# Row softmax in one arena: one queue with tiles that grow from 3 to 31 rows, and GpSimd in place of SyncE waiting for the last stores

## The chip, the cores and the metric

The kernel runs on one core of one Trainium2 chip. The metric is the time on the device in microseconds (us). Before the change it was 163.44 us (median of 3 runs, 163.35 to 163.72). Profiled spans are about 1.8 us shorter than these times, because they run from the first to the last instruction of the core.

## The reference

```python
batch, seq, dim = 16, 1024, 512            # x: float32
x_scaled = x / 2.0
x_max = np.max(x_scaled, axis=-1, keepdims=True)
exp_x = np.exp(x_scaled - x_max)
return exp_x / np.sum(exp_x, axis=-1, keepdims=True)
```

These are 16384 rows of 512 values. On 128 partitions each partition has 128 rows of 2 KB. The input and the output are 33.55 MB each; nothing can be left out of the 67.11 MB that pass the DMA engines.

## The kernel before

A "tile" is one load and, later, one store of r rows on each partition, so one packet of r x 2 KB per partition. Its chunks are the pieces that VectorE and ScalarE work on. A tile's second number is its place in the arena of on-chip memory. A tile whose place overlaps an earlier tile's is loaded late, when that tile's store has landed.

```python
PLAN = [
    ([3], 0), ([4, 3], 3), ([5] * 3, 10), ([5] * 3, 25), ([5] * 3, 40), ([5] * 3, 55),
    ([5] * 3, 70), ([5] * 3, 85), ([5] * 3, 10), ([4, 3], 3), ([3], 0), ([3], 25),
]
ARENA = 100
LAG = 2
# ... (cut)
    def do_max(k):                              # VectorE: one reduce per chunk, waits for the load
        # ...
        )._wait_ge(ld[t], 16).then_inc(s_max, 1)
    def do_mul(k):                              # VectorE: reciprocal, then one multiply per row
        # ...
    def compute_and_store():
        # ... ScalarE: one exp per row, with the row's sum
        for k in range(len(chunks) + LAG):
            if k < len(chunks):
                do_max(k)
            if k >= LAG:
                do_mul(k - LAG)

        late = sorted(behind)
        for t in range(len(tiles)):
            nc.sync.wait_ge(s_mul, last_chunk[t] + 1)
            nc.sync.dma_start(out=dram(of, t), in_=sb(t)).then_inc(st[t], 16)
            while late and max(behind[late[0]]) <= t - 1:
                u = late.pop(0)
                for v in behind[u]:
                    nc.sync.wait_ge(st[v], 16)
                nc.sync.dma_start(out=sb(u), in_=dram(xf, u)).then_inc(ld[u], 16)
        for t in range(len(tiles)):
            nc.sync.wait_ge(st[t], 16)
```

All 24 DMAs (12 loads, 12 stores) go through SyncE's queue in program order. The first eight loads (100 rows) are issued at once; stores queue behind them.

The softmax here doesn't subtract the row's maximum and nothing guards it: scores larger than these inputs give would overflow.

Of the kernel before, what the change touches and what calls it, by code (L numbers as in the profile page):

```python
# [1 line left out]

# [4 lines left out]




PLAN = [
    ([3], 0), ([4, 3], 3), ([5] * 3, 10), ([5] * 3, 25), ([5] * 3, 40), ([5] * 3, 55),
    ([5] * 3, 70), ([5] * 3, 85), ([5] * 3, 10), ([4, 3], 3), ([3], 0), ([3], 25),
]
ARENA = 100
LAG = 2


@with_exitstack
def kernel(  # L20
    ctx: ExitStack,
    tc: tile.TileContext,
    x: bass.AP,
    out: bass.AP,
):
    nc = tc.nc
    fp32 = mybir.dt.float32

    xf = x.flatten_outer_dims()
    of = out.flatten_outer_dims()  # L30
    N, D = xf.shape
    P = nc.NUM_PARTITIONS
    n_rows = N // P
    assert sum(sum(c) for c, _ in PLAN) == n_rows

    arena = nc.alloc_sbuf_tensor("arena", (P, ARENA, D), fp32)
    negmax = nc.alloc_sbuf_tensor("negmax", (P, n_rows), fp32)
    sums = nc.alloc_sbuf_tensor("sums", (P, n_rows), fp32)
    recip = nc.alloc_sbuf_tensor("recip", (P, n_rows), fp32)



    tiles, chunks, base = [], [], 0
    for t, (cs, at) in enumerate(PLAN):
        r = sum(cs)
        tiles.append((base, r, at))
        o = 0
        for c in cs:
            chunks.append((t, base + o, c, at + o))
            o += c  # L50
        base += r
    last_chunk = {c[0]: k for k, c in enumerate(chunks)}

    def dram(ap, t):
        b, r, _ = tiles[t]
        return ap[b * P : (b + r) * P].rearrange("(p r) d -> p r d", r=r)

    def sb(t):
        _, r, at = tiles[t]
        return arena[:, at : at + r, :]  # L60


    behind = {}
    for t, (_, r, at) in enumerate(tiles):
        for u in range(t):
            _, ru, au = tiles[u]
            if at < au + ru and au < at + r:
                behind.setdefault(t, []).append(u)

    ld = [tc.alloc_semaphore(f"ld{t}") for t in range(len(tiles))]  # L70
    st = [tc.alloc_semaphore(f"st{t}") for t in range(len(tiles))]
    s_max = tc.alloc_semaphore("s_max")
    s_exp = tc.alloc_semaphore("s_exp")
    s_rec = tc.alloc_semaphore("s_rec")
    s_mul = tc.alloc_semaphore("s_mul")



    def issue_loads(begin, end):
        for t in range(begin, end):  # L80
            if t not in behind:
                nc.sync.dma_start(out=sb(t), in_=dram(xf, t)).then_inc(ld[t], 16)

    def do_max(k):
        t, b, c, a = chunks[k]
        nc.vector.reduce_max(  # L86
            out=negmax[:, b : b + c],
            in_=arena[:, a : a + c],
            axis=mybir.AxisListType.X,
            negate=True,  # L90
        )._wait_ge(ld[t], 16).then_inc(s_max, 1)

    def do_mul(k):
        t, b, c, a = chunks[k]
        nc.vector.reciprocal(  # L95
            out=recip[:, b : b + c], in_=sums[:, b : b + c]
        )._wait_ge(s_exp, k + 1).then_inc(s_rec, 1)
        for r in range(c):
            ins = nc.vector.tensor_scalar_mul(  # L99
                out=arena[:, a + r],  # L100
                in0=arena[:, a + r],
                scalar1=recip[:, b + r : b + r + 1],
            )
            if r == 0:
                ins._wait_ge(s_rec, k + 1)
        ins.then_inc(s_mul, 1)

    def compute_and_store():

        for k, (t, b, c, a) in enumerate(chunks):  # L110
            for r in range(c):
                ins = nc.scalar.activation(  # L112
                    out=arena[:, a + r],
                    in_=arena[:, a + r],
                    func=mybir.ActivationFunctionType.Exp,
                    bias=negmax[:, b + r : b + r + 1],
                    scale=0.5,
                    accum_out=sums[:, b + r : b + r + 1],
                )
                if r == 0:  # L120
                    ins._wait_ge(s_max, k + 1)
            ins.then_inc(s_exp, 1)
# [5 lines that stand above are left out]
            if k >= LAG:  # L128
                do_mul(k - LAG)

        late = sorted(behind)
        for t in range(len(tiles)):
            nc.sync.wait_ge(s_mul, last_chunk[t] + 1)
            nc.sync.dma_start(out=dram(of, t), in_=sb(t)).then_inc(st[t], 16)
            while late and max(behind[late[0]]) <= t - 1:
                u = late.pop(0)
                for v in behind[u]:
                    nc.sync.wait_ge(st[v], 16)
                nc.sync.dma_start(out=sb(u), in_=dram(xf, u)).then_inc(ld[u], 16)
        for t in range(len(tiles)):  # L140
            nc.sync.wait_ge(st[t], 16)



    hook = nc.inst_callbacks[-1]
    nc.remove_inst_callback(hook)
    symbolic = nc._always_lower_symbolic_ap
    nc._always_lower_symbolic_ap = False
    here = str(nc.cur_bb)
    entry = nc.main_func.blocks[0]  # L150
    head, jumps = entry.instructions[:-5], entry.instructions[-5:]
    entry.instructions = []
    nc.switch_bb("main", None)
    issue_loads(0, 2)
    first = list(entry.instructions)
    at = next(k for k, i in enumerate(head) if type(i).__name__ == "InstDrain")
    entry.instructions = head[:at] + first + head[at:]
    issue_loads(2, len(tiles))
    compute_and_store()
    entry.instructions = list(entry.instructions) + jumps  # L160
    nc.switch_bb(here, None)
    nc._always_lower_symbolic_ap = symbolic
    nc.push_inst_callback(hook)


# [1 line left out]
_INS = ['x']  # L167
_OUTS = [((16, 1024, 512), 'float32')]


# [23 lines left out]
```

## Time and profile before

| | before |
|---|---|
| time, median | 163.44 us |
| profiled span | 161.6 us |
| VectorE / ScalarE busy | 126.1 / 94.5 us |
| DMA moved | 67.14 MB, mean 416 GB/s |
| DMA packets | 3460 |

From the profile page of the kernel before. The rows of digits are 40 slices of the span, each the busy tenths of 4.04 us; GB/s is what the DMA engines moved in that slice. Below them are the chain of work that ended last and one group of instructions (count, busy time, mean ns of one, idle time before them and what ended it).

```profile
span 161.6 us, 513 instructions
...
## 2 busy tenths in 40 slices
DVE  0484599999999999999999999999999999100000
...
DMA  7999999999999997999999899999999999999992
GB/s 291 465 403 449 441 418 464 395 458 395 464 411 436 449 411 254 444 438 472 418 434 464 388 431 406 445 456 388 461 441 456 395 464 395 464 411 456 390 410 90
DMA packets 3460, 67.14 MB, mean 416 GB/s; under 512 B 385, under 2 KB 385, under 8 KB 1153
...
## 4 chain that ended last, share of the span: by engine, by line
DVE 74%; DMA 10%; issue 0%; DVEq 0%
...
L86 DVE TENSOR_REDUCE negmax<-arena 128x5 f32<-128x2560 f32 (+2 forms) x28 | 72.3, 2586 | 10.8 <-DMA arena<-in_x_dram 10.8
```

The DMA row is at 9 almost throughout, while VectorE stops before the end (the zeros at the right of its row). The windows view says how fast the DMA is. Its columns are the stretch, its length, busy time of VectorE, ScalarE and GpSimd, the TensorE clock, DMA share and GB/s.

```profile
32.00:58.00 26.00, 25.82 (x36) 19.20 (x54) 0.00 (x0) 1.00 1.01 433
57.00:65.00 8.00, 7.93 (x12) 5.42 (x15) 0.00 (x0) 1.00 0.94 336
70.00:100.00 30.00, 29.79 (x44) 22.25 (x63) 0.00 (x0) 1.00 1.00 430
100.00:140.00 40.00, 37.49 (x63) 26.20 (x72) 0.00 (x0) 1.00 1.01 436
140.00:155.00 15.00, 0.00 (x0) 0.00 (x0) 0.00 (x0) 1.00 0.97 416
158.00:160.00 2.00, 0.00 (x0) 0.00 (x0) 0.00 (x0) 1.00 0.22 89
```

The three longest stretches are at 430 to 436 GB/s. The stretch 140:155 reads 416; the view counts a packet whole at its start, and on the median engine a store of 15 rows landed 9.07 us after the one before it (141.48 and 150.55 us), which is 434 GB/s there too. The stretch 57:65 is slower, and the last 2 us before 160 hold only stragglers. The Trainium skill ("DMA: Bandwidth & Descriptors", Specifications) gives 435 GB/s as the ceiling of the fabric, and this trace lies on it. So the DMA queue is the limit.

The chain of waits has another answer, and must be read with care. These are its last pieces (start, length, what):

```profile
137.06 0.40 DVEq L189
137.45 0.40 DVE arena L99
```

It ends at 137.85 us, although the span is 161.6 us. The chain follows instructions, and the last instruction that counts as work is VectorE's. The 24 us of stores after it are in no chain.

The trace also records when each of the 16 DMA engines finished its part of a DMA ("landing"). For the last store the median engine landed at 158.49 us and the last one at 160.48 us. The remaining 1.09 us is SyncE's wait and the closing barrier of all engines.

### The profile page before, as it was taken

The numbers are of one execution on the slowest core, as the hardware profiler recorded it, in microseconds if no ns is written. First come the engines' busy times: TensorE is split into PE (matmuls) and PEld (weight loads), VectorE is DVE, ScalarE is ACT, GpSimd is POOL, SyncE is SP. The second block draws the span as 40 slices with busy tenths as digits, with TensorE's granted clock in tenths as the row PEclk, the third lists the DMA queues.
The fourth block names the chain that finished last, engine by engine and source line by source line (L and its number), as shares of the span: only waits on it lengthen the run. The fifth ranks groups of instructions, "written<-read, shape, count | busy, mean of one in ns | idle before, by whom it ended". The sixth has DMA issues, their size and how long they took to land.

```text
span 161.6 us, 513 instructions
## 1 busy us (share of the span) xinstructions
DVE 126.1 (78%) x184; ACT 94.5 (59%) x257; POOL 0.2 (0%) x4
## 2 busy tenths in 40 slices
DVE  0484599999999999999999999999999999100000
ACT  3439087866688666797666886667978655000000
POOL 0000000000000000000000000000000000000000
DMA  7999999999999997999999899999999999999992
GB/s 291 465 403 449 441 418 464 395 458 395 464 411 436 449 411 254 444 438 472 418 434 464 388 431 406 445 456 388 461 441 456 395 464 395 464 411 456 390 410 90
DMA packets 3460, 67.14 MB, mean 416 GB/s; under 512 B 385, under 2 KB 385, under 8 KB 1153
## 3 DMA queue, kind: packets, MB, share of 16 engines
q1 hardware_dynamic: 3456, 67.11, 97.7%
q14 instruction: 4, 0.02, 0.0%
HBM read 33.55 MB, written 33.55 MB: 415 GB/s over the span
## 4 chain that ended last, share of the span: by engine, by line
DVE 74%; DMA 10%; issue 0%; DVEq 0%
DVE negmax L86 40%; DVE arena L99 32%; DMA arena<-in_x_dram 10%; DVE recip L95 2%; DVEq L189 0%
## 5 line engine op out<-in xcount | busy, mean ns | idle before, releaser
L112 ACT ACTIVATE arena<-arena,negmax 128x512 f32<-128x512 f32 x128 | 90.7, 710 | 40.1 <-DVE negmax L86 40.1
L86 DVE TENSOR_REDUCE negmax<-arena 128x5 f32<-128x2560 f32 (+2 forms) x28 | 72.3, 2586 | 10.8 <-DMA arena<-in_x_dram 10.8
L99 DVE TENSOR_SCALAR arena<-arena,recip 128x512 f32<-128x512 f32 x128 | 53.2, 482 | 1.0
L112 ACT ACTIVATION_READ_ACCUMULATOR arena<-arena,negmax 128x1 f32 x128 | 23.9, 187 | 0.0
L95 DVE RECIPROCAL recip<-sums 128x5 f32<-128x5 f32 (+2 forms) x28 | 5.0, 177 | 0.0
L112 ACT ACT_TABLE_LOAD x1 | 1.3, 1283 | 1.3 <-PEq L178 1.3
L178 POOL MEMSET const-bfloat16-1.0<- 128x1 bf16 x1 | 0.1, 101 | 0.0
L178 POOL MEMSET const-uint8-127<- 128x1 uint8 x1 | 0.1, 101 | 0.0
L178 POOL MEMSET const-float32-0.0<- 128x1 f32 x1 | 0.1, 98 | 0.2 <-issue 0.2
L178 POOL MEMSET const-float32-1.0<- 128x1 f32 x1 | 0.1, 98 | 0.0
## 6 DMA issues: line engine op xcount, KB each, us to landing
arena<-in_x_dram SPq DMA_DIRECT2D x7, 3840.0 KB, 33.7
out_dram<-arena SPq DMA_DIRECT2D x7, 3840.0 KB, 33.2
arena<-in_x_dram SPq DMA_DIRECT2D x2, 1792.0 KB, 15.2
out_dram<-arena SPq DMA_DIRECT2D x2, 1792.0 KB, 33.2
arena<-in_x_dram SPq DMA_DIRECT2D x3, 768.0 KB, 23.5
out_dram<-arena SPq DMA_DIRECT2D x3, 768.0 KB, 22.6
```

The lines of the kernel that those rows point to most:

```text
L86: nc.vector.reduce_max(out=negmax[:, b : b + c], in_=arena[:, a : a + c], axis=mybir.AxisListType.X, negate=True,)._wait_ge(ld[t], 16).the ...
L95: nc.vector.reciprocal(out=recip[:, b : b + c], in_=sums[:, b : b + c])._wait_ge(s_exp, k + 1).then_inc(s_rec, 1)
L99: ins = nc.vector.tensor_scalar_mul(out=arena[:, a + r], in0=arena[:, a + r], scalar1=recip[:, b + r : b + r + 1],)
L112: ins = nc.scalar.activation(out=arena[:, a + r], in_=arena[:, a + r], func=mybir.ActivationFunctionType.Exp, bias=negmax[:, b + r : b + r ...
L178: nc = _bacc.Bacc("TRN2", target_bir_lowering=False, num_devices=1)
```

## The change

The intent, as it can be read from the change: fewer and larger DMAs (18 instead of 24), tiles that grow so that VectorE's early loads come in time, a written-out queue order, two larger late tiles instead of four small ones, and a shorter end, as the engine that leads the closing barrier waits itself.

```diff
 PLAN = [
-    ([3], 0), ([4, 3], 3), ([5] * 3, 10), ([5] * 3, 25), ([5] * 3, 40), ([5] * 3, 55),
-    ([5] * 3, 70), ([5] * 3, 85), ([5] * 3, 10), ([4, 3], 3), ([3], 0), ([3], 25),
+    ([3], 0), ([5], 3), ([5, 4], 8), ([5] * 3, 17), ([7] * 3, 32), ([8, 8, 8, 7], 53),
+    ([5] * 3, 84), ([6, 6, 5], 0), ([4] * 3, 17),
 ]
-ARENA = 100
+ARENA = 99
+QUEUE = [
+    ("load", 0), ("load", 1), ("load", 2), ("load", 3), ("load", 4), ("load", 5),
+    ("load", 6), ("store", 0), ("store", 1), ("store", 2), ("store", 3), ("load", 7),
+    ("store", 4), ("load", 8), ("store", 5), ("store", 6), ("store", 7), ("store", 8),
+]
 ... (cut: do_queue walks this list on SyncE: a load waits for the stores it lies behind, a store for
      its last chunk; stores that no load waits for share one semaphore, s_end)
-        for t in range(len(tiles)):
-            nc.sync.wait_ge(st[t], 16)
+    for u, sem in [*st.items(), ("end", s_end)]:
+        nc.gpsimd.wait_ge(sem, stored[u])
```

More of the change, by code (lines that the diff above doesn't have):

```diff
@@ L11 @@
 PLAN = [
-    ([3], 0), ([4, 3], 3), ([5] * 3, 10), ([5] * 3, 25), ([5] * 3, 40), ([5] * 3, 55),
-    ([5] * 3, 70), ([5] * 3, 85), ([5] * 3, 10), ([4, 3], 3), ([3], 0), ([3], 25),
+    ([3], 0), ([5], 3), ([5, 4], 8), ([5] * 3, 17), ([7] * 3, 32), ([8, 8, 8, 7], 53),
+    ([5] * 3, 84), ([6, 6, 5], 0), ([4] * 3, 17),
 ]
-ARENA = 100
+ARENA = 99
 LAG = 2
+QUEUE = [
[3 more added lines that the diff above has]
+]
+EARLY = 2
 @with_exitstack
@@ L51 @@
         base += r
-    last_chunk = {c[0]: k for k, c in enumerate(chunks)}
     def dram(ap, t):
@@ L68 @@
                 behind.setdefault(t, []).append(u)
+    awaited = {u for us in behind.values() for u in us}
     ld = [tc.alloc_semaphore(f"ld{t}") for t in range(len(tiles))]
-    st = [tc.alloc_semaphore(f"st{t}") for t in range(len(tiles))]
+    st = {t: tc.alloc_semaphore(f"st{t}") for t in sorted(awaited)}
+    s_end = tc.alloc_semaphore("s_end")
     s_max = tc.alloc_semaphore("s_max")
@@ L75, with do_queue @@
     s_mul = tc.alloc_semaphore("s_mul")
-    def issue_loads(begin, end):
-        for t in range(begin, end):
-            if t not in behind:
-                nc.sync.dma_start(out=sb(t), in_=dram(xf, t)).then_inc(ld[t], 16)
+    stored = {}
+    loads_of = {}
+    for kind, t, *rest in QUEUE:
+        if kind == "load":
+            loads_of[t] = loads_of.get(t, 0) + 16 * (len(rest[2]) if rest else 1)
+    def do_queue(items):
+        for kind, t, *rest in items:
+            b, r, at = tiles[t]
+            lo, hi, groups = rest if rest else (0, r, [(0, P)])
+            if kind == "load":
+                for u in behind.get(t, []):
+                    nc.sync.wait_ge(st[u], stored[u])
+                for p, q in groups:
+                    nc.sync.dma_start(
+                        out=arena[p:q, at + lo : at + hi, :], in_=dram(xf, t)[p:q, lo:hi]
+                    ).then_inc(ld[t], 16)
+                continue
+            k = max(k for k, c in enumerate(chunks) if c[0] == t and c[1] - b < hi)
+            nc.sync.wait_ge(s_mul, k + 1)
+            for p, q in groups:
+                u = t if t in awaited else "end"
+                nc.sync.dma_start(
+                    out=dram(of, t)[p:q, lo:hi], in_=arena[p:q, at + lo : at + hi, :]
+                ).then_inc(st[t] if t in awaited else s_end, 16)
+                stored[u] = stored.get(u, 0) + 16
     def do_max(k):
@@ L90, in do_max @@
             negate=True,
-        )._wait_ge(ld[t], 16).then_inc(s_max, 1)
+        )._wait_ge(ld[t], loads_of[t]).then_inc(s_max, 1)
     def do_mul(k):
@@ L106, in do_mul, with do_compute @@
         ins.then_inc(s_mul, 1)
-    def compute_and_store():
+    def do_compute():
         for k, (t, b, c, a) in enumerate(chunks):
@@ L129, in compute_and_store @@
                 do_mul(k - LAG)
-        late = sorted(behind)
-        for t in range(len(tiles)):
-            nc.sync.wait_ge(s_mul, last_chunk[t] + 1)
-            nc.sync.dma_start(out=dram(of, t), in_=sb(t)).then_inc(st[t], 16)
-            while late and max(behind[late[0]]) <= t - 1:
-                u = late.pop(0)
-                for v in behind[u]:
-                    nc.sync.wait_ge(st[v], 16)
-                nc.sync.dma_start(out=sb(u), in_=dram(xf, u)).then_inc(ld[u], 16)
-        for t in range(len(tiles)):
-            nc.sync.wait_ge(st[t], 16)
     hook = nc.inst_callbacks[-1]
@@ L153 @@
     nc.switch_bb("main", None)
-    issue_loads(0, 2)
+    do_queue(QUEUE[:EARLY])
     first = list(entry.instructions)
@@ L157 @@
     entry.instructions = head[:at] + first + head[at:]
-    issue_loads(2, len(tiles))
-    compute_and_store()
+    do_compute()
+    do_queue(QUEUE[EARLY:])
+    for u, sem in [*st.items(), ("end", s_end)]:
+        nc.gpsimd.wait_ge(sem, stored[u])
     entry.instructions = list(entry.instructions) + jumps
```

## The prediction

> **What bounds the kernel now.** The DMA engines. In the page's 40 slices DMA stands at 9 tenths from the second slice to the 39th; the windows view gives 430 to 436 GB/s in each long stretch (32:58, 70:100, 100:140). The Trainium skill, "DMA: Bandwidth & Descriptors", Specifications, puts the fabric ceiling at 435 GB/s; this trace sits on it. Its packet records agree: packets of 6144, 14336 and 30720 bytes start 230, 532 and 1134 ns apart on an engine, a line of 27.2 bytes/ns (16 engines: 435 GB/s) plus 4 ns a packet. At that rate 67.11 MB alone take 154.3 us.
>
> The chain of waits names VectorE for 74%, but it ends at 137.85 us; after that only stores run. The groups give VectorE 126.1 us busy plus 10.8 us of waiting for loads, ScalarE 94.5. Neither is the limit.
>
> Outside the 154.3 us: 1.0 us before the first packet; about 1.2 us of slow packets at 60 to 63 us (slice 15: 254 GB/s, cause unknown to me); overhead per DMA; the slowest of the 16 engines ends 2.1 us after the median one (158.0 to 160.16); 1.1 us from the last landing (160.48) through SyncE's wait and the closing barrier to 161.57.
>
> **What the change does.**
> - 24 DMAs become 18, bytes unchanged. With 8 packets per engine at 4 ns and a semaphore packet of 9 ns, a DMA costs about 0.045 us beyond its bytes: 0.3 us saved, all on the path (estimate).
> - The late 3-row loads go. Near them, at 103 and 115 us, some packets were 0.1 to 0.2 us late and the slowest engine's lag grew. Worth 0 to 0.4 us.
> - GpSimd waits for the last stores itself. Before, SyncE's last wait ended at 160.50 and GpSimd went on at 160.81. About 0.15 us of that goes, on the path.
> - Growing tiles change VectorE's early waits (8.9 us for 10.8, estimate) and its chunks from 28 to 23. It ends near 134 us instead of 138. Off the path: worth nothing.
>
> **Does the DMA queue run dry?** I worked out the schedule with durations from the trace (max 0.533 us a row + 0.06, multiply 0.414 a row + 0.13, DMA 0.61 a row); the same sum gives before's DMA end as 157.7 (median engine 158.0). In the changed kernel the 17-row load is issued at about 74 us for a start at 82, the 21-row store 74 for 92, the 12-row load 83 for 105, the 31-row store 97 for 112, the last three 113, 127, 135 for 131, 140, 150. Smallest margin 8 us: no holes, and no late load.
>
> **Predicted:** 162.8 us, range 161.8 to 163.6. Faster by over 2%: 0.02; within 2%: 0.96; slower by over 2%: 0.02.
>
> **Right** would be: about 2,600 DMA packets instead of 3,460; long windows still at 430 to 437 GB/s; VectorE ends 3 to 4 us earlier while the span shrinks by under 1 us; about 0.9 us from last landing to end. **Wrong:** a slice of low GB/s between 70 and 150 us (queue dry); another rate for packets of 63,488 bytes; VectorE waiting for a load after 60 us.
>
> **What would make it wrong.** If the slow packets near 60 us belong to the last 15-row load rather than to the first switch from loads to stores, they may vanish (161.7). If very large packets are slower, or spread the engines' finish further than 2 us, the time can rise by 1 to 2 us. A gain over 2% is all but excluded: only some 7 us lie outside the bytes.

## The result and the profile after

The changed kernel takes 163.16 us (median of 4 runs, 162.92 to 163.25); before, on the same chip, 163.46 us (163.35 to 163.72). The ratio is 0.9977, 95% interval 0.996 to 0.9995. Ratios here and below are the mean time of one kernel's fast runs over that of the other's fast runs of the same rounds, so not quite the ratio of the medians. The runs below come from several batches, in which before's own median was 163.16 to 163.68 us, so kernels are compared by their ratios to before.

The same lines of the changed kernel's page:

```profile
span 161.1 us, 494 instructions
...
## 2 busy tenths in 40 slices
DVE  0557989999999999999999999999999994000000
...
DMA  7999999997996998999999989899899979999991
GB/s 264 458 476 397 458 404 480 450 490 331 504 473 286 458 397 292 458 433 458 419 413 458 480 382 491 363 416 552 349 457 489 426 340 458 409 439 415 420 464 61
DMA packets 2595, 67.13 MB, mean 417 GB/s; under 512 B 288, under 2 KB 288, under 8 KB 544
...
## 4 chain that ended last, share of the span: by engine, by line
DVE 69%; DMA 13%; issue 0%; DVEq 0%; SPq 0%
...
L115 DVE TENSOR_REDUCE negmax<-arena 128x5 f32<-128x2560 f32 (+5 forms) x23 | 71.7, 3116 | 9.0 <-DMA arena<-in_x_dram 9.0
```

Its windows:

```profile
32.00:58.00 26.00, 25.86 (x31) 20.38 (x58) 0.00 (x0) 1.00 1.00 434
57.00:65.00 8.00, 7.96 (x10) 5.71 (x17) 0.00 (x0) 1.00 0.97 351
70.00:100.00 30.00, 29.82 (x43) 21.30 (x60) 0.00 (x0) 1.00 1.01 434
100.00:140.00 40.00, 34.58 (x58) 24.44 (x68) 0.00 (x0) 1.00 1.00 432
140.00:155.00 15.00, 0.00 (x0) 0.00 (x0) 0.00 (x0) 1.00 1.00 430
158.00:160.00 2.00, 0.00 (x0) 0.00 (x0) 0.00 (x0) 1.00 0.09 37
```

And the end of its chain, which again is VectorE's end and not that of the span:

```profile
133.68 0.40 DVEq L209
134.07 0.79 DVE arena L128 x2
```

The packets fell by a quarter, the rate in the long stretches did not move (434, 434, 432 and 430 GB/s), packets of 63,488 bytes took 2.342 us (27.2 bytes/ns beyond the 0.234 us of a 6,144-byte packet, the same line as before), the hole at 57 to 65 us is still there, and VectorE ends at 134.86 us, 3.0 us earlier, with 9.0 us of waiting for loads instead of 10.8. When the queue got its work can be read from SyncE's timeline of the changed kernel (start, length from the first to the last of the group, what):

```profile
17.31 31.70 SPq L108 DMA_DIRECT2D out_dram<-arena  x4
74.94 0.34 SPq L100 DMA_DIRECT2D arena<-in_x_dram  x1
75.32 0.81 SPq L108 DMA_DIRECT2D out_dram<-arena  x1
83.95 0.34 SPq L100 DMA_DIRECT2D arena<-in_x_dram  x1
96.94 38.28 SPq L108 DMA_DIRECT2D out_dram<-arena  x4
```

Worked out for the prediction were 74, 74, 83 and 97 us for the DMAs that stand here at 74.94, 75.32, 83.95 and 96.94. The queue never ran dry: the store ahead of the first late load landed at 82.90 us on the median engine, 8.0 us after that load's issue.

The end of the span, from the trace's landings of the last store, in us:

| kernel | waits at the end | median engine lands | last engine lands | span ends | last landing to end |
|---|---|---|---|---|---|
| before | SyncE | 158.49 | 160.48 | 161.57 | 1.09 |
| the change | GpSimd | 158.24 | 160.09 | 161.14 | 1.05 |

So the profiled 0.43 us are 0.25 us on the median engine, 0.14 us of spread, and 0.04 us at the end.

### The profile page after: what moved, and what is told of

The parts are those of the page before. It is cut to its first block, busy times and chain, and to the rows that moved or that the text cites. A ratio compares the mean times of both kernels' runs of the same rounds, so it can differ in the third digit from the quotient of the medians.

```text
span 161.1 us, 494 instructions
## 1 busy us (share of the span) xinstructions
DVE 125.1 (78%) x174; ACT 94.0 (58%) x257; POOL 0.2 (0%) x4
## 4 chain that ended last, share of the span: by engine, by line
DVE 69%; DMA 13%; issue 0%; DVEq 0%; SPq 0%
DVE negmax L115 38%; DVE arena L128 30%; DMA arena<-in_x_dram 13%; DVE recip L124 1%; DVEq L209 0%; SPq L100 0%
## 5 line engine op out<-in xcount | busy, mean ns | idle before, releaser
L115 DVE TENSOR_REDUCE negmax<-arena 128x5 f32<-128x2560 f32 (+5 forms) x23 | 71.7, 3116 | 9.0 <-DMA arena<-in_x_dram 9.0
L124 DVE RECIPROCAL recip<-sums 128x5 f32<-128x5 f32 (+5 forms) x23 | 4.2, 181 | 0.0
```

What stands on the lines that cost most here:

```text
L115: nc.vector.reduce_max(out=negmax[:, b : b + c], in_=arena[:, a : a + c], axis=mybir.AxisListType.X, negate=True,)._wait_ge(ld[t], loads_o ...
L124: nc.vector.reciprocal(out=recip[:, b : b + c], in_=sums[:, b : b + c])._wait_ge(s_exp, k + 1).then_inc(s_rec, 1)
```

## Experiments

All twelve kernels below gave the right result.

### Who waits at the end: plan_sync and before_pool

plan_sync is the change with the final waits on SyncE; before_pool is the kernel before with them on GpSimd.

```diff
-        nc.gpsimd.wait_ge(sem, stored[u])       # plan_sync, from the change
+        nc.sync.wait_ge(sem, stored[u])
-            nc.sync.wait_ge(st[t], 16)          # before_pool, from before
+            nc.gpsimd.wait_ge(st[t], 16)
```

> The tile plan of the change, with SyncE waiting for the last stores as before. If the hand-over from SyncE to GpSimd cost what I predicted (0.15 us), this run is 0.15 us slower than the whole change (163.3 against 163.16) and the stretch from the last landing to the end of the span is about 1.1 us. The trace of the change already shows 1.05 us there against 1.09 before, so the rival says: equal within 0.05 us, the wait's engine does not matter.

> The plan of before, with GpSimd waiting for the last stores. Predicted theory: 0.15 us under before. Rival: as before within 0.05 us, so that all of the gain of 0.3 us is the plan's.

Measured: plan_sync 163.41 us, ratio to before 0.9987 (0.9971 to 1.0004); before_pool 163.68 us, ratio 1.0003 (0.9984 to 1.0022). The times alone can't tell 0.15 us from nothing. The traces can: from the last landing to the end of the span plan_sync took 1.03 us and before_pool 1.11 us, next to 1.05 (change) and 1.09 (before). The rival is right. In plan_sync 0.34 us pass from the last landing (160.57) to GpSimd's step in the barrier (160.91); with GpSimd waiting, in the change, 0.34 us as well (160.09 to 160.44), because GpSimd then runs its own branch and drain there. The hand-over did not go; GpSimd's own steps took its place. What differs between the two plans is later: GpSimd's instruction that clears the semaphores took 0.184 us in both traces of the old plan and 0.136 us in both of the new one, which has fewer semaphores (0.117 us in plan15, 0.222 us in probe with its 16 more). That accounts for the 0.04 us at the end.

### What one more DMA costs: split3 and split3_loads

split3 cuts the change's stores, split3_loads its loads, into pieces of at most 3 rows. Bytes and order stay.

```diff
+            for lo in range(0, r, 3):                                  # of each store, or each load
+                yield kind, t, lo, min(lo + 3, r), [(0, P)]
```

> The change with its nine stores cut into pieces of at most three rows: 45 stores, 54 DMAs instead of 18, the same bytes and the same order. If a DMA costs about 0.045 us beyond its bytes and the queue stays full, 36 more cost 1.6 us: about 164.8 us. If the overhead hides behind other engines' packets, 163.2. If each DMA bore a fixed cost of a microsecond or more in the queue, it would be over 190.

> The change with its nine loads, instead of its stores, cut into pieces of at most three rows: 44 loads, 53 DMAs, 35 more than the change. The cut stores cost 2.4 us for 36 DMAs (0.05 us each on the median engine, 0.07 us on the engine that ends last). If a DMA costs the same whichever way it goes, 1.8 to 2.5 us more than the change: 165.0 to 165.7 us. If only stores pay for their count, about 163.2 us, and the merged late loads of the change were worth nothing.

Measured: split3 165.75 us, ratio 1.0141 (1.0117 to 1.0166); split3_loads 163.90 us, ratio 1.0016 (0.9999 to 1.0034). Windows of split3, then of split3_loads:

```profile
32.00:57.00 25.00, 24.86 (x31) 19.86 (x57) 0.00 (x0) 1.00 1.02 439
...
100.00:140.00 40.00, 34.53 (x58) 24.38 (x68) 0.00 (x0) 1.00 1.01 421
```

```profile
32.00:57.00 25.00, 24.86 (x33) 19.86 (x57) 0.00 (x0) 1.00 1.02 417
57.00:65.00 8.00, 7.96 (x10) 5.72 (x17) 0.00 (x0) 1.00 1.02 419
```

Where cut stores run (100:140) the rate is 421 GB/s instead of 432; where cut loads run (32:57) it is 417 instead of 434. A piece of 3 rows is 786,432 bytes. Most slices of split3's end show 422 to 426 GB/s:

```profile
GB/s 275 445 474 383 458 498 357 485 517 419 326 496 370 443 368 294 424 425 426 422 471 425 386 422 423 441 471 330 416 425 426 422 424 425 425 423 422 426 420 71
```

At 425 GB/s a piece takes 1.85 us and at 417 GB/s 1.886 us, against 1.81 us at 435; the landings on the median engine agree (1.85 us from store to store, 1.88 us from load to load). So a store costs about 0.04 us and a load about 0.08 us beyond its bytes, in a queue that is never empty. The predicted 0.045 us was right for stores and too low for loads.

The whole times need two more terms: the slow stretch, and the lag of the last engine behind the median one. split3 lost 0.0164 x 163.5 = 2.7 us against the change by the ratios, more than the 1.6 us expected. In its trace the median engine (the last landing of each engine counted once) landed at 160.07 us instead of 158.24, 1.8 us later, as 36 stores at 0.04 to 0.05 us should; the last engine landed at 162.65 instead of 160.09, so the lag had grown by another 0.7 us. split3_loads lost 0.6 us by the ratios for 35 DMAs, less than expected. 35 loads at 0.08 us are 2.8 us; but the slow stretch at 57 to 65 us is gone in it (419 GB/s, the same as around it; 0.10 us of the "excess" defined below, instead of 1.23), which leaves 1.7 us. The median engine did land 1.63 us later (159.87 us). The last engine's lag was 1.27 us instead of 1.85, so the last landing came only 1.05 us later. Nobody had named either reason. Both expectations missed in size.

### The slow packets near 60 us: early_store, warm_first, warm_third, cut_last_load

The measure for these runs: for every packet its time above the median of its size, added up in a stretch and divided by the 16 engines ("excess"). Before has 1.28 us of it between 57 and 65 us, the change 1.23 us.

early_store moves the first store ahead of the 21-row load:

```diff
-    ("load", 0), ("load", 1), ("load", 2), ("load", 3), ("load", 4), ("load", 5),
-    ("load", 6), ("store", 0), ("store", 1), ...
+    ("load", 0), ("load", 1), ("load", 2), ("load", 3), ("store", 0), ("load", 4), ("load", 5),
+    ("load", 6), ("store", 1), ...
```

> The change with its first store moved ahead of the 21-row load, so that the first switch from loads to stores comes near 21 us instead of 61 us. If the slow packets at 59 to 62 us come from the first switch from loads to stores, they now appear at about 19 to 22 us and the stretch at 60 us is at full rate; time the same within 0.3 us. If they come from the time or from the last load, they stay at about 60 us. If a full queue of waiting stores causes them, they vanish or shrink and the time falls by up to 1.2 us.

Measured: 163.25 us, ratio 0.9975 (0.9958 to 0.9993). Its windows:

```profile
17.00:20.00 3.00, 2.96 (x5) 3.00 (x9) 0.00 (x0) 1.00 1.01 369
20.00:23.00 3.00, 1.84 (x5) 2.60 (x8) 0.00 (x0) 1.00 0.82 262
57.00:65.00 8.00, 7.96 (x12) 5.72 (x17) 0.00 (x0) 1.00 0.97 416
```

The excess moved whole: 1.14 us between 17 and 26 us, 0.00 between 57 and 65, where the rate is 416 GB/s instead of 351. So it moves with the first switch of the queue from loads to stores, and belongs neither to the clock time nor to the last load; and moving it gains nothing. The time is the change's.

warm_first and warm_third put a copy of 64 KB from input to output in front of all loads, or behind the second; the first store waits for it and writes its bytes again.

```diff
+    ("warm", 0), ("load", 0), ("load", 1), ...        # warm_first
+    ("load", 0), ("load", 1), ("warm", 0), ...        # warm_third
+            if kind == "warm":
+                nc.sync.dma_start(out=of[0:128, 0:128], in_=xf[0:128, 0:128]).then_inc(s_warm, 16)
```

> The change with one 64 KB copy from the input to the output in front of all loads (its bytes are written again by the first store, which waits for it). If the 1.2 us of slow packets belong to the first write to the output whatever is around it, they no longer appear at 59 to 62 us, and come at the start instead: time about as the change, or up to 1 us less if the start hides them. If they belong to the turn of the queue from loads to SBUF-to-HBM stores, they stay at 59 to 62 us and the time is 0.2 to 0.6 us above the change.

> The same copy behind the first two loads, so that it starts near 6 us, with the fabric already busy. First-write theory: slow packets of about 1.2 us an engine near 5 to 7 us and none at 59 to 62 us; time as the change within 0.4 us. Turn theory: slow packets stay at 59 to 62 us; time 0.2 to 0.4 us above the change.

Measured: warm_first 164.55 us, ratio 1.006 (1.004 to 1.008); warm_third 164.17 us, ratio 1.0037 (1.0018 to 1.0056). Neither theory holds alone. The excess at 57 to 65 us fell to 0.47 us and 0.28 us, so an earlier copy to the output takes away most of it. But it did not end: excess at 88 to 97 us, at the next turn from a load to a store, rose from 0.11 (0.25 in plan_sync, with the same queue) to 0.47 and 0.41 us, and the copy itself delayed the loads (in warm_third the third load landed 0.9 us later than in the change, 13.26 against 12.38 us on the median engine). Both are slower than the change, by 1.4 and 1.0 us by the ratios, which neither expectation had. In warm_third that is the last engine's lag: the median engine landed the last store at 158.36 us (158.24 in the change), the last one at 161.72 us (160.09). Why the copy leaves such a lag was not tried.

cut_last_load asks whether the size of the packets before the first store matters, as split3_loads had suggested:

```diff
-    ("load", 6), ("store", 0), ...
+    ("load", 6, 0, 3, ...), ("load", 6, 3, 6, ...), ... ("load", 6, 12, 15, ...), ("store", 0), ...
```

> The change with only the last load before the first store (15 rows) cut into five of 3 rows: 22 DMAs. When all loads were cut, the slow packets at 57 to 65 us were gone (0.09 us of excess on the mean engine instead of 1.23), and 1.0 us of the 1.6 us that 35 more DMAs cost came back. If it is the size of the packets just before the first store that makes them slow, this run has under 0.3 us of excess there and takes about 162.4 us (1.0 us gained, 4 DMAs at 0.05 to 0.07 us lost): ratio to before about 0.993. If it was the cutting of the earlier loads, or the later issue of the stores, the excess stays near 1.2 us and the time is about 163.4 us.

Measured: 163.09 us, ratio 0.9996 (0.9974 to 1.0018; before was at 163.16 us in this batch). The excess at 57 to 65 us is 1.03 us, and the last piece of the load took 2.65 us on the median engine where the others took 1.88. The size of the packets just before the first store is not the cause. Why the stretch is gone when all loads are cut stays open. split3_loads also issued its first store later, at 47.66 us instead of 17.31, but that alone does not explain it: its store then waited about 17 us for its turn, while early_store's waited about 4 us and had the excess.

### Is VectorE on the path: vector_plus9 and vector_plus24

Each adds max instructions on VectorE whose results nobody uses: two of 8 rows (8.7 us), or six (24.1 us).

```diff
             if k < len(chunks):
+                if k in (10, 11):                     # vector_plus24: (7, 8, 9, 10, 11, 12)
+                    ... nc.vector.reduce_max(out=junk[...], in_=arena[...]) ...
                 do_max(k)
```

> The change with two more max instructions of 8 rows on VectorE (4.33 us each, results unused), near 70 us: 8.7 us more VectorE work. If VectorE is off the path, as predicted, the time stays at 163.2 within 0.3 us and VectorE ends near 143 us. If the chain of waits, which gives VectorE 69% of the span, named the limit, the time rises by about 8.7 us.

> The same with six more max instructions (7, 7, 8, 8, 8, 7 rows: 24.1 us). The 31-row store is then issued near 121 us and the queue in front of it ends near 113, so it runs dry: about 8 to 10 us longer, 171 to 173 us, with slices of low GB/s near 113 to 121. If the slack were not 14 to 16 us but none, it would be 187; if it were over 24, 163.

Measured: vector_plus9 163.60 us, ratio 1.000 (0.997 to 1.0029), VectorE's end at 143.4 us; vector_plus24 173.67 us, ratio 1.0614 (1.0577 to 1.065). The first is 0.4 us above the change, 0.1 us outside what was expected, though the intervals of the two ratios overlap. Its DMA row is as full as the change's to the end of VectorE's longer work, and its last landing (160.35 us) is 0.26 us later than the change's, less than between the change and plan_sync (160.57 us), which have the same queue:

```profile
DVE  0557989999999999999999999999999999950000
...
DMA  7999999997997998999999989899899979999991
```

The second's DMA row and windows show where the slack ends:

```profile
DMA  7999989997998989999999999910699989769995
...
100.00:112.00 12.00, 11.96 (x17) 9.70 (x28) 0.00 (x0) 1.00 1.00 427
113.00:122.00 9.00, 8.96 (x17) 6.51 (x19) 0.00 (x0) 1.00 0.01 4
122.00:140.00 18.00, 17.89 (x23) 12.38 (x35) 0.00 (x0) 1.00 1.05 451
```

Between 113 and 122 us VectorE is fully busy and the DMA engines move 4 GB/s: the 31-row store is not ready and the queue has nothing else. VectorE's slack is thus more than 9 and less than 24 us. By the packet records no packet was under way from 114.14 to 122.18 us, and again from 150.26 to 152.56, when the store before the last was late (the 7 and 6 near the right of the DMA row). Together that is 10.3 us, which is what the run lost against the change (10.4 us by the ratios, 0.7 us beyond the time expected); so about 14 of the 24.1 us were slack (estimate). A side result: after the first dry stretch the 16 engines landed the 31-row store within 0.20 us of each other, and after the second the last store within 0.23 us, instead of 2.1 us in the change. So the lag went when the queue was empty, and did not come back in the stores that followed.

### Which engine ends last: probe

The last row of the last store goes out as 16 small stores of 1, 2, ... 15 and 8 partitions, each with its own semaphore.

```diff
-    ("store", 7), ("store", 8),
+    ("store", 7), ("store", 8, 0, 11, [(0, 128)]),
+    ("store", 8, 11, 12, [(0, 1), (1, 3), (3, 6), (6, 10), ... (105, 120), (120, 128)]),
```

> The change with the last row of the last store sent as 16 small stores of 1, 2, ... 15 and 8 partitions, each with a semaphore of its own. By the Trainium skill a store of k partitions uses the k lowest of the 16 engines. The landing of the store with k partitions should step up by 1 to 2 us at the k that first takes in the engine that ends last. If no engine is always last, there is no step. The time does not matter here; up to 2 us longer.

Measured: one run, 165.87 us. The last landing of the store with k partitions:

```
k            1       2       3       4       5       6       7       8      15
lands us  158.15  159.50  159.68  160.74  160.93  161.12  161.30  161.48  162.75
```

There are two steps, 1.36 us at k = 2 and 1.06 us at k = 4; every other k adds 0.2 us or less. The Trainium skill ("DMA: Bandwidth & Descriptors", Why a DMA increments its semaphore by 16 and not by 1) says that a DMA from SyncE with k partitions, for the k used here, runs on the k lowest engines. The trace shows k landings for each of these stores, which agrees; it does not number the engines. Read with the page, the steps are the engines of number 1 and 3 (counted from 0).

But the last landing of each store hides an engine that is late and enters at a larger k. All landings can be followed from store to store, as each one adds about 0.18 us on an engine. Just before, the large part of the last store (11 rows) had landed last at 160.55, 159.95, 159.74, 159.31 and 158.44 us, on the other engines by 158.09. Engine 3 fits the first of these, engine 14 the third, engine 1 the fourth and engine 13 the fifth. The one left, 159.95 us, must be engine 15, which takes part in none of the small stores. So in this one trace the late engines are 3, 15, 14 and 1 in this order. The expected test, a step of the last landing, could not show 14 and 15. Whether the same engines are late in other runs was not tried.

### Still fewer DMAs: plan15

```diff
 PLAN = [
+    ([3], 0), ([5, 4], 3), ([6, 6, 5], 12), ([5, 5, 6], 29), ([8, 8, 8, 7], 45),
+    ([6, 6, 6, 5], 76), ([6, 6, 6, 6, 5], 0),
 ]
 QUEUE = [
+    ("load", 0), ("load", 1), ("load", 2), ("load", 3), ("load", 4), ("load", 5),
+    ("store", 0), ("store", 1), ("store", 2), ("store", 3), ("load", 6),
+    ("store", 4), ("store", 5), ("store", 6, 0, 18, [(0, 128)]), ("store", 6, 18, 29, [(0, 128)]),
 ]
```

> A plan with still fewer DMAs: tiles of 3, 9, 17, 16, 31, 23 rows, one late tile of 29 rows in the place of the first three, its store in two pieces: 15 DMAs, 3 fewer than the change and 9 fewer than before. VectorE waits longer for its early loads (16 us instead of 9, worked out) and ends near 141 us instead of 134.9; the last store but one is issued near 137 us for a start at 140, its last piece at 141 for 151: no dry queue. If a DMA costs 0.05 to 0.07 us and VectorE is off the path: 0.45 to 0.65 us under before, ratio about 0.9965, and the median engine ends about 0.15 us earlier than with the change (near 157.65 us). If VectorE's early waits count, as the chain of waits has it, about 6 us longer.

Measured: 162.38 us (162.30 to 162.49), ratio 0.9939 (0.9926 to 0.9953). It beats both kernels, and before by more than expected (1.0 us by the ratio). From its page and its waits:

```profile
span 160.5 us, 489 instructions
...
## 2 busy tenths in 40 slices
DVE  0459099999999999999999999907999999950000
...
DMA  8999999997999896999999989999899989999892
...
DMA packets 2163, 67.13 MB, mean 418 GB/s; under 512 B 240, under 2 KB 240, under 8 KB 496
```

```profile
DVE negmax L116 <- DMA arena<-in_x_dram: 17.0, 4, 4.9
```

VectorE waits 17.0 us for loads, nearly twice as long as in the change (4.9 of them near 107 us, for the late load, which nobody had expected), and ends at 142.6 us, 7.7 us later; yet the kernel is faster. That is the plainest sign that those waits cost nothing. But the gain is not where it was expected: the median engine landed the last store at 158.21 us (158.24 in the change), while the last one landed at 159.49 us (160.09). The last landing is 0.60 us earlier, nearly all of it less lag of the last engine behind the median one (1.28 us instead of 1.85; in plan_sync, early_store, cut_last_load and vector_plus9 it was 1.73 to 2.24). This plan has one late load, so its queue goes from loads to stores twice, where the change's does so three times. In the change the lag of the last engine behind the median grew from 1.35 us (last load before the stores) to 1.71 us at the first late load; in plan15 from 1.24 to 1.29 us. That the number of such turns is the cause fits these two traces but was not tried by itself, and it can't be all: split3_loads turns three times as well, and ended with a lag of 1.27 us.

## Why the prediction was right or wrong

- **The DMA queue bounds the kernel: right.** All long stretches stayed at 430 to 434 GB/s; 8.7 us more VectorE work left the DMA row full, and the 0.4 us between the medians is not clear of the noise; 24 us made the queue dry and cost 10 us.
- **VectorE's time and early waits are worth nothing: right.** It ended 3.0 us earlier in the change for no gain, and 7.7 us later in plan15, which is faster.
- **No dry queue, 8 us of margin: right.** The late DMAs were issued within 1.4 us of the worked-out times.
- **Six DMAs fewer save 0.3 us: right in size.** The median engine landed 0.25 us earlier (0.18 us from before_pool to plan_sync, the other pair of traces with these two plans). By the cut runs, three loads at 0.08 us and three stores at 0.04 us make 0.36 us. The gain on the clock is 0.30 us by the medians, 0.38 us by the ratio.
- **The late 3-row loads, 0 to 0.4 us: mis-sized.** The excess at 97 to 120 us was 0.07 us before and 0.06 us after (0.22 and 0.02 us in before_pool and plan_sync). The last engine's lag at the end was 1.99 and 2.15 us in the two traces of the old plan, and 1.85 and 2.24 us in the two of the new one with the same queue. No gain can be told from these; and in split3_loads, with many 3-row late loads, the lag at the end was no larger (1.27 us).
- **"About 0.15 us of that goes, on the path": wrong.** This is the step that failed. From the last landing to the end it was 1.05 us, not 0.9, against 1.09 before; with the engines exchanged it was 1.03 us (plan_sync) and 1.11 us (before_pool). From the last landing to GpSimd's step in the barrier 0.33 to 0.34 us passed in all four: GpSimd's branch and drain took as long as the hand-over had.
- **The slow packets stay if they belong to the first switch: right.** They stayed, and early_store moved them with the first store. Why they come with the first store, and why cutting all loads removes them, stays open.

The predicted gain was 0.64 us, the measured one 0.30 us; the two terms that gave little or nothing (0.2 and 0.15 us) are the difference. The clock alone can't settle this: the interval of the ratio allows a gain of 0.1 to 0.65 us, and it is the traces that tell the terms apart. The range, 161.8 to 163.6 us, also held the time before the change, so that it came true does not test these small terms. What "within 2%" rests on, and what the runs confirm, is the bound, read from the DMA rate and not from the chain of waits.

## What to carry to other kernels

When the DMA engines run at their ceiling from start to end, count what lies outside the bytes (first packet, first switch from loads to stores, cost per DMA, spread of the engines' ends, closing barrier) before judging a change; here that was about 7 us, and VectorE's earlier end (3.0 us) did not touch it. Trade VectorE's early waits for fewer DMAs and fewer late loads as long as the queue has work in front of every store. Before moving a wait to another engine to save a hand-over, add up what that engine itself does between its wait and the barrier.

## What the Trainium skill lacked or had wrong

- "DMA: Bandwidth & Descriptors", Anatomy of one DMA — SWDGE (gpsimd) path: for DMAs that GpSimd issues it fits one DMA as about 2.0 us plus its bytes. In SyncE's queue, never empty, one more DMA here cost 0.04 us (store) to 0.08 us (load). The page does not give this marginal cost.
- The same page, Bandwidth: its rule, under a table of DMAs that GpSimd issued, asks for 1 MiB and more for 75% of peak. It does not say what a full queue does: pieces of 768 KB queued back to back by SyncE ran at 417 to 425 GB/s, 96 to 98% of 435.
- The same page, Where 436 GB/s comes from: it says that about 358 GB/s of HBM bind a transfer between HBM and on-chip memory, next to its own 425 GB/s for a single core; that 358 GB/s is the share when both cores of the HBM stream stands in the section before. With one core running, loads alone ran at 433 and 434 GB/s (32:58) and loads and stores mixed at 430 to 436 GB/s; what held was the 435 GB/s of the fabric.
- The same page, Latency and other measured facts: it names engines 7 and 15 as usually the slower ones and ties that to descriptors written by GpSimd. Here, with all DMAs issued by SyncE, the one trace of probe has engines 3, 15, 14 and 1 late (2.7 to 1.5 us behind the median engine), and engine 7 among the others. The numbers rest on the page's rule of the k lowest engines.
- No page has the slow stretch at the first switch from loads to stores: 1.0 to 1.35 us of excess per engine, once, moving with the first store (0.28 and 0.47 us behind an early copy, 0.10 us in split3_loads).
